# Windowed attention in a two-layer hybrid decoder: values computed with tokens on partitions, a shared tile pool, a constant kept on chip and an earlier end of the query step

## The chip, the cores and the metric

The kernel runs on one core of one Trainium2 chip. The metric is the device time of one execution in microseconds; three runs of the kernel before are known, and one more execution was profiled.

## The reference

One inference step of two layers. Each layer normalises its input, projects it with one weight matrix, and gives the parts to two groups of heads: windowed attention (8 query heads of 64, 2 key/value heads, window 128, a sink per head) and a gated delta rule (4 heads of 128 by 128). Their outputs are gated, concatenated and projected back, and the input is added. It does this for a prompt of 2048 tokens and for 8 sample sequences of 4 tokens with caches, all in float32. What the change touches is this:

```python
def _sink_attend(q, k, v, mask, sinks):
    s = einsum('...qkgd,...skd->...kgqs', q, k) * HEAD_DIM ** -0.5
    s = where(mask, s, -inf)
    m = maximum(max(s, -1), sink)
    p = exp(s - m)
    denom = sum(p, -1) + exp(sink - m)
    return einsum('...kgqs,...skd->...qkgd', p / denom, v)
```

For the prompt, a block of 128 queries sees its own block of 128 keys up to the diagonal and the previous block above the diagonal, 128 keys in all for each query; the first block of the sequence has no previous one.

## The kernel before, in words

The prompt's 2048 tokens are worked through in groups of 512 (`gi` 0 to 3), each with 4 token tiles of 128, for each of 2 layers. A group's body is a run of projections (`block`, line 484): each takes 8 or 4 pieces of weights and makes, with three float32r passes, 24 matmuls of 512 columns per output tile. Between pieces, `tk.step()` advances side tasks. Such a task is a Python generator with a number of turns and a start and an end step in the dictionary `W`: `q_task` (steps 17 to 30, 6 turns), `inv_rows` (from step 20, 33 turns, GpSimd's row by row inversion of small triangular blocks, lines 811 and 813, copied out at 817), `att_task` (24 to 47, 20 turns), `inv_task`, `qk_task`, `scan_task`, `mixd_task`, `mixa_task`. So the emitted order of work is set by these steps; a scheduler that allots tiles and places semaphores then lays down each engine's queue before the run. On the chip each queue is worked in order.

Tiles come from pools of equal buffers. `f2` gives 2 KB per partition and has 9 of them; the masked probabilities `PT`, the tanh `th`, the products `pr` of `inv_rows`, the sample's temporaries and many others live there. `f4` gives 4 KB and has 5: the raw queries `qh` (two, held until the last query transposes), `At` of `inv_rows`, the probabilities `Pt`, the inverse's `X`, `Xc`, `T2` and others. PSUM has 4 tiles for projections (`mm`) and 4 for everything else (`px`).

Weights: `fetch` (line 244) keeps 4 pieces ahead. In the first group of a layer a piece is loaded whole into `raw` (its own pool of 3, line 258 with its DMA in 259), split into a rounded half by ScalarE (line 262) and a rest by GpSimd (line 263), and written out for the other groups, which load the two halves (line 265). In the first group the sample's rows are multiplied with the same `raw` piece (line 519); in the third group the output weights are loaded whole once more for this.

Attention for a token tile `tt`, in turns: `scores(tt, 0)` makes the scores of four heads (lines 668, 669), ScalarE copies the own block's part to `Pt` and VectorE fills in the previous block's part above the diagonal (672, 673), so that `Pt` holds, for each query, its 128 keys of two blocks in one row of 128; `scores(tt, 1)` the other four; `softmax` takes the maximum, the exponentials (689) and the denominators, and multiplies `Pt` with their reciprocals (696). `turn` transposes the four heads of a key/value head on TensorE (701) and makes two masked copies on VectorE (704), one for the own block's keys and one for the previous block's. `values` multiplies with the value tiles (711):

```python
for kb in range(1 if head else 0, 2):
    for kv in range(2):
        PE.matmul(po[kv * HD:kv * HD + HD, :], vts[tt + kb][:, kv * HD:kv * HD + HD],
                  PT[kv, kb].rearrange("p a b -> p (a b)"), ...)
A.copy(g["m0"][tt // 2][:, tt % 2], po.rearrange("p (a b) -> p a b", a=4))
```

The value tile (128 keys by 64) is the stationary operand and the probabilities of four heads (512 columns) move; the result has channels on partitions, the two key/value heads on two halves of them, which is how the gate (1027) and the output projection want it. The turns of tile `tt` lie between those of tile `tt + 1`.

A sample head (`sample_head`) loads a selection matrix `sel` (128 by 256, float32) for itself, 8 times in all (line 1272), for the matmul in line 1300.

## Time and profile before

| | us |
|---|---|
| median of 3 runs | 2385.9 (2383.13 to 2389.49) |
| the profiled execution | 2384.89 |
| its span | 2383.1 |
| granted TensorE clock, mean | 0.972 |

PE is TensorE's matmuls, PEld its weight loads, DVE VectorE, ACT ScalarE, POOL GpSimd, SP the engine that issues the DMAs. "L711" is a line of the kernel before. A row of the timeline gives the start, the length of the merged stretch, the operation with what it writes and reads, how many, and in brackets the idle time of the engine before it with what ended it. A row of a group gives how many, the busy time in us, the mean ns of one, and the idle time before them. A float32 matmul that is no transpose shows as two instructions, each with its own weight load.

### The profile page before, as it was taken

To read this page: it belongs to the slowest core of one execution; us is meant where nothing else is said; L and a number is where in the kernel's file an instruction comes from. 1 tells how busy PE (TensorE), PEld (TensorE's weight loads), DVE (VectorE), ACT (ScalarE), POOL (GpSimd) and SP (SyncE) were. 2 spreads that over 40 slices of the span, in tenths; PEclk is the share of its full clock that TensorE was granted. 3 is DMA by queue.
4 is the path that set the end of the run, shared out by engine and by line. 5 is a ranking of instruction groups with operands and counts; after the bars stand their busy time and mean duration, and the time that the engine had idled before them with its cause. 6 is when DMAs were issued, how large, how long until landed. Compare 5 with 4: busy or idle time off the path is not lost.

```text
span 2383.1 us, 41057 instructions
## 1 busy us (share of the span) xinstructions
PE 2227.7 (93%) x14340; PEld 1771.6 (74%) x14340; DVE 1642.2 (69%) x5060; ACT 909.6 (38%) x2864; POOL 447.4 (19%) x732
## 2 busy tenths in 40 slices
PE   6989999879999899979999899999899989999799
PEld 5766788658887687867877677887688777788677
DVE  6677677577678764677656867778767787557663
ACT  3544523234233342334325445244432344323331
POOL 3272320400004000040023623104000130002100
PEclk9989999979999999989999999999999999999899
DMA  5654685514765348544566546854357534675236
GB/s 172 208 190 160 206 282 184 158 57 140 225 194 170 105 146 267 181 124 131 162 213 222 173 148 215 272 190 125 118 162 224 192 113 133 200 231 161 82 116 199
DMA packets 211298, 414.14 MB, mean 174 GB/s; under 512 B 61340, under 2 KB 89604, under 8 KB 211028
## 3 DMA queue, kind: packets, MB, share of 16 engines
q1 hardware_dynamic: 211092, 411.53, 53.4%
q8 instruction: 113, 1.85, 0.3%
q14 instruction: 93, 0.76, 0.1%
HBM read 312.84 MB, written 101.62 MB: 174 GB/s over the span
## 4 chain that ended last, share of the span: by engine, by line
PE 59%; DVE 8%; POOL 6%; DMA 3%; issue 2%; ACT 2%; SPq 0%; POOLq 0%; ACTq 0%; DVEq 0%
PE mm L484 40%; POOL Xh L813 3%; POOL pr L811 3%; PE px L711 2%; PE px L946 1%; PE px L954 1%; PE px L940 1%; PE px L926 1%; PE px L934 1%; PE px L701 1%; PE px L781 1%; DMA hl<-hl 1%; PE px L668 1%; PE px L519 1%; DVE vT L744 1%
## 5 line engine op out<-in xcount | busy, mean ns | idle before, releaser
L484 PE MATMUL mm<-xT,hl 128*128 128x512 f32 x3072 | 777.5, 403 | 4.1 <-POOL hl L263 3.8
L484 PEld LDWEIGHTS mm<-xT,hl 128*128 128x128 f32 x3072 | 571.0, 192 | 124.2 <-issue 6.7
L484 PE MATMUL mm<-hl,xT 128*128 128x512 f32 (+1 forms) x2304 | 511.2, 369 | 44.3 <-DVE rs_t L204 25.9
L484 PEld LDWEIGHTS mm<-hl,xT 128*128 128x128 f32 x2304 | 379.1, 192 | 114.4 <-issue 56.5
L263 POOL TENSOR_TENSOR hl<-raw,hl 128x512 fp32r<-128x512 f32 (+1 forms) x144 | 186.5, 1300 | 409.7 <-ACT hl L262 360.2
L811 POOL TENSOR_TENSOR pr<-At,Xh 128x126 f32<-128x126 f32 (+22 forms) x248 | 99.2, 400 | 580.1 <-DMA At<-ad 286.6
L484 PE MATMUL mm<-mixA,hl 128*128 128x512 f32 x768 | 187.9, 397 | 0.0
L484 PE MATMUL mm<-mixD,hl 128*128 128x512 f32 x768 | 181.6, 392 | 1.0 <-DVE mixD L970 1.0
L1029 POOL TENSOR_TENSOR mixA<-m,mixA 128x256 fp32r<-128x256 f32 x64 | 45.5, 736 | 719.2 <-ACT mixA L1028 492.7
L484 PEld LDWEIGHTS mm<-mixD,hl 128*128 128x128 f32 x768 | 142.6, 188 | 33.7 <-DVE mixD L970 1.8
L744 DVE SCALAR_TENSOR_TENSOR KQ<-mm,pc,KQ 128x511 f32<-128x511 f32 (+2 forms) x192 | 142.0, 740 | 35.1 <-ACT KQ L741 34.8
L484 PEld LDWEIGHTS mm<-mixA,hl 128*128 128x128 f32 x768 | 140.7, 188 | 30.4 <-issue 2.2
L262 ACT CAST hl<-raw 128x512 fp32r<-128x512 f32 (+1 forms) x144 | 85.0, 595 | 140.2 <-PE mm L484 76.4
L689 ACT ACTIVATE Pt<-Pt,nm 128x128 f32<-128x128 f32 x256 | 99.3, 391 | 21.5 <-DVE nm L681 21.5
L813 POOL TENSOR_TENSOR Xh<-Xh,pr 128x126 f32<-128x126 f32 (+22 forms) x248 | 103.0, 416 | 18.9
L1060 DVE TENSOR_TENSOR xr<-mm,xr 128x512 f32<-128x512 f32 x64 | 43.7, 691 | 79.6 <-PE mm L484 79.6
L672 ACT COPY Pt<-px 128x256 f32<-128x256 f32 x128 | 43.7, 374 | 143.1 <-PE px L669 110.8
L704 DVE TENSOR_TENSOR PT<-px,cst 128x512 f32<-128x512 f32 x124 | 82.1, 683 | 16.7 <-PE px L701 16.2
L701 PE MATMUL px<-cst,Pt 128*128 128x128 f32 x256 | 41.9, 289 | 41.2 <-ACT th L210 26.9
L741 ACT ACTIVATE KQ<-mm,pc 128x512 f32<-128x512 f32 x64 | 43.7, 687 | 94.0 <-PE mm L484 93.9
L668 PE MATMUL px<-kT,q 128*128 128x256 f32 (+1 forms) x256 | 72.6, 313 | 5.0 <-DVE q L650 1.7
L359 ACT CAST xT<-x 128x512 fp32r<-128x512 f32 x64 | 35.5, 618 | 93.9 <-PE mm L484 83.0
(392 smaller groups left out, 3708.7 us busy)
## 6 DMA issues: line engine op xcount, KB each, us to landing
hl<-hl SPq DMA_DIRECT2D x512, 512.0 KB
hl<-hl SPq DMA_DIRECT2D x64, 264.0 KB
raw<-in_wf_dram SPq DMA_DIRECT2D x64, 256.0 KB
raw<-in_w_out_dram SPq DMA_DIRECT2D x64, 256.0 KB
x<-in_x_prompt_dram SPq DMA_DIRECT2D x16, 512.0 KB
raw<-in_wt_dram SPq DMA_DIRECT2D x32, 256.0 KB
xr<-in_x_prompt_dram SPq DMA_DIRECT2D x32, 256.0 KB
y<-xr SPq DMA_DIRECT2D x32, 256.0 KB
```

What stands on the lines that cost most here:

```text
L262: A.copy(hl[:, 0], raw)
L263: G.tensor_sub(hl[:, 1], raw, hl[:, 0].bitcast(F32))
L484: PE.matmul(pss[u], lhs, rhs, start=(k == 0 and q == 0), stop=(k == 7 and q == 2))
L668: PE.matmul(sps[kv][:, jj, c0:], q, kT[:, kv, cols], start=True, stop=False)
L689: A.activation(Pt[:, kv, j], Pt[:, kv, j], AF.Exp, bias=nm[:, h:h + 1], scale=0.125, accum_out=den[:, h:h + 1])
L701: PE.transpose(pt[:, j, :], Pt[:, kv, j], ident)
L704: V.tensor_mul(ptt, pt, (umat if kb else slower).unsqueeze(1).to_broadcast([P, 4, P]))
L711: PE.matmul(po[kv * HD:kv * HD + HD, :], vts[tt + kb][:, kv * HD:kv * HD + HD], PT[kv, kb].rearrange("p a b -> p (a b)"), start=(kb == 0 o ...
L744: V.scalar_tensor_tensor(dest[:, d:], ps[:, 0:T - d], w, dest[:, d:], op0=ALU.mult, op1=ALU.add)
L811: G.tensor_mul(pr, At[:, j, j + 1:].unsqueeze(2).to_broadcast([P, n, m]), Xh[:, j, 0:m].unsqueeze(1).to_broadcast([P, n, m]))
L813: G.tensor_sub(Xh[:, j + 1:, 0:m], Xh[:, j + 1:, 0:m], pr)
L1029: G.tensor_sub(lo, m, hi.bitcast(F32))
```

## The change

Five edits. (1) The whole weight pieces `raw` come from the `f2` pool, which has 12 buffers instead of 9; the pool of 3 is gone. (2) `sel` is loaded once into a constant tile. (3) `q_task` runs from step 18 to 27 instead of 17 to 30. (4) `softmax` no longer multiplies `Pt`; it returns the reciprocals. `turn` makes the own block's masked copy on VectorE as before, but the previous block's part as a plain copy by ScalarE less the masked copy, subtracted on GpSimd. `values` takes the transposed probabilities of one head (128 by 128) as the stationary operand and the value tile's 64 columns as the moving one, so that the result has tokens on partitions; VectorE multiplies it with the reciprocals on the way out of PSUM; `finish` transposes it to channels on partitions on TensorE and ScalarE copies it to `m0`. (5) The values of tile `tt - 2` are emitted right after the first scores of tile `tt`, and `finish` after its second scores and softmax; there are still 20 turns.

```diff
-W = dict(k1=8, pre0=13, pre1=19, q0=17, q1=30, ir0=20, ir1=((32,) + (27,) * 3), iv0=(36, 31, 31, 31), iv1=(41, 36, 36, 36), att0=24, att1=47,
-         qk0=29, qk1=35, sc0=(41,) * 4, sc1=52, sa0=-4, sa1=30, sp0=20, sp1=50, sh0=58, shd=11, shl=13, wla=4, wraw=3, xn0=2, xn1=8, sla=3,
+W = dict(k1=8, pre0=13, pre1=19, q0=18, q1=27, ir0=20, ir1=((32,) + (27,) * 3), iv0=(36, 31, 31, 31), iv1=(41, 36, 36, 36), att0=24, att1=47,
+         qk0=29, qk1=35, sc0=(41,) * 4, sc1=52, sa0=-4, sa1=30, sp0=20, sp1=50, sh0=58, shd=11, shl=13, wla=4, xn0=2, xn1=8, sla=3,
...
     def f2(shape, dt=F32, name="f2"):
-        return f2p.tile(shape, dt, tag="f2", name=name, bufs=9)
+        return f2p.tile(shape, dt, tag="f2", name=name, bufs=12)
...
+    sel = cp.tile([P, 2, P], F32, name="sel")
...
                 if whole:
-                    raw = wp.tile([P, kk, m], F32, tag="raw", name="raw", bufs=W["wraw"])
+                    raw = f2([P, kk, m], name="raw")
                     dma(raw, src)
...
-                rd = smt([P, 8], "rd")
+                rd = smt([P, 8], "rd", 3)
                 V.reciprocal(rd, den)
-                for kv in range(2):
-                    V.tensor_mul(Pt[:, kv], Pt[:, kv], rd[:, 4 * kv:4 * kv + 4].unsqueeze(2).to_broadcast([P, 4, P]))
+                return rd
 
             def turn(tt, Pt, kv, PT):
                 pt = xt_([P, 4, P])
                 for j in range(4):
                     PE.transpose(pt[:, j, :], Pt[:, kv, j], ident)
-                for kb in range(1 if gi == 0 and tt == 0 else 0, 2):
-                    ptt = PT[kv, kb] = f2([P, 4, P], name="PT")
-                    V.tensor_mul(ptt, pt, (umat if kb else slower).unsqueeze(1).to_broadcast([P, 4, P]))
-
-            def values(tt, PT):
+                if gi or tt:
+                    pp = PT[kv, 0] = f2([P, 4, P], name="PT")
+                    A.copy(pp, pt)
+                po = PT[kv, 1] = f2([P, 4, P], name="PT")
+                V.tensor_mul(po, pt, umat.unsqueeze(1).to_broadcast([P, 4, P]))
+                if gi or tt:
+                    G.tensor_sub(pp, pp, po)
+
+            def values(tt, PT, rd):
                 head = gi == 0 and tt == 0
-                po = xt_([P, T])
-                for kb in range(1 if head else 0, 2):
-                    for kv in range(2):
-                        PE.matmul(po[kv * HD:kv * HD + HD, :], vts[tt + kb][:, kv * HD:kv * HD + HD],
-                                  PT[kv, kb].rearrange("p a b -> p (a b)"), start=(kb == 0 or head), stop=(kb == 1))
+                po = xt_([P, 4, 2, HD])
+                for kv in range(2):
+                    for j in range(4):
+                        for kb in range(1 if head else 0, 2):
+                            PE.matmul(po[:, j, kv], PT[kv, kb][:, j], vts[tt + kb][:, kv * HD:kv * HD + HD], start=(kb == 0 or head),
+                                      stop=(kb == 1))
+                o = f2([P, 4, 2, HD], name="o")
+                V.tensor_mul(o, po, rd.rearrange("p (k j) -> p j k", k=2).unsqueeze(3).to_broadcast([P, 4, 2, HD]))
+                return o
+
+            def finish(tt, o):
+                pt = xt_([P, 4, P])
+                for j in range(4):
+                    PE.transpose(pt[:, j], o[:, j].rearrange("p a d -> p (a d)"), ident)
                 if tt % 2 == 0:
                     g["m0"].append(gp.tile([P, 2, 4, P], F32, tag="q", name="m0", bufs=5))
-                A.copy(g["m0"][tt // 2][:, tt % 2], po.rearrange("p (a b) -> p a b", a=4))
+                A.copy(g["m0"][tt // 2][:, tt % 2], pt)
 
-            last = None
-            for tt in range(NT + 1):
+            Pts, PTs, rds = {}, {}, {}
+            for tt in range(NT + 2):
                 if tt < NT:
-                    Pt = f4([P, 2, 4, P], name="Pt")
-                    scores(tt, 0, Pt)
-                    yield
-                if last is not None:
-                    turn(tt - 1, last, 0, PT)
+                    Pts[tt], PTs[tt] = f4([P, 2, 4, P], name="Pt"), {}
+                    scores(tt, 0, Pts[tt])
+                if tt > 1:
+                    o = values(tt - 2, PTs[tt - 2], rds[tt - 2])
+                yield
+                if 0 < tt <= NT:
+                    turn(tt - 1, Pts[tt - 1], 0, PTs[tt - 1])
                     yield
                 if tt < NT:
-                    scores(tt, 1, Pt)
-                    softmax(Pt)
+                    scores(tt, 1, Pts[tt])
+                    rds[tt] = softmax(Pts[tt])
+                if tt > 1:
+                    finish(tt - 2, o)
+                yield
+                if 0 < tt <= NT:
+                    turn(tt - 1, Pts[tt - 1], 1, PTs[tt - 1])
                     yield
-                if last is not None:
-                    turn(tt - 1, last, 1, PT)
-                    yield
-                    values(tt - 1, PT)
-                    yield
-                last, PT = Pt, {}
...
-        sel = f2([P, 2, P], name="sel")
-        dma(sel, a["const_k"])
...
     dma(cs_s, a["const_s"])
+    dma(sel, a["const_k"])
```

## Rows read from the trace of the kernel before

**Rows 1.** The page, part 1: busy us, share, instructions

```profile
PE 2227.7 (93%) x14340; PEld 1771.6 (74%) x14340; DVE 1642.2 (69%) x5060; ACT 909.6 (38%) x2864; POOL 447.4 (19%) x732
```

**Rows 2.** Windows: busy us of PE, PEld, DVE, ACT, POOL; granted clock, DMA

```profile
400.00:500.00 100.00, 81.51 (x453) 63.69 (x453) 67.00 (x213) 32.22 (x106) 25.84 (x64) 0.86 0.42 128
...
1000.00:1100.00 100.00, 84.19 (x580) 68.14 (x579) 73.46 (x207) 37.80 (x119) 25.63 (x64) 0.93 0.38 112
...
0.00:2384.00 2384.00, 2227.70 (x14340) 1771.62 (x14340) 1642.16 (x5060) 909.61 (x2864) 447.40 (x732) 0.97 0.54 174
```

**Rows 3.** Waits of TensorE: us in total, times, longest us

```profile
PE px L701 <- ACT th L210: 26.9, 2, 13.5
PE mm L484 <- DVE rs_t L204: 25.9, 7, 5.5
PE mm L484 <- issue: 13.2, 3, 8.0
...
PE px L701 <- DVE Pt L696: 9.6, 3, 6.3
...
PE px L912 <- DVE vT L211: 5.8, 2, 4.9
...
PE mm L484 <- POOL hl L263: 3.8, 1, 3.8
```

**Rows 4.** Timeline of TensorE: one token tile's values (start us, us)

```profile
499.54 1.94 PE L711 MATMUL px<-PT,vt 128*64 128x512 f32 x8
501.41 0.46 PE L1193 MATMUL px<-cst,xx 56*128 56x56 f32 x4
```

**Rows 5.** Timeline of TensorE: nearest shapes to the new matmuls

```profile
617.97 0.94 PE L337 MATMUL px<-ones,xsq 128*128 128x1 f32 x8
...
497.42 1.06 PE L898 MATMUL px<-KQ 128*128 128x128 f32 x8
...
509.36 1.14 PE L864 MATMUL px<-Xc,AK 64*64 64x64 f32 x16
...
539.18 0.60 PE L701 MATMUL px<-cst,Pt 128*128 128x128 f32 x4
```

**Rows 6.** Groups of TensorE by shape: busy us, mean ns, idle before

```profile
L898 PE MATMUL px<-KQ 128*128 128x128 f32 x256 | 35.4, 282 | 2.8 <-ACT junk L895 1.7 <-ACT Xc L858 1.0
...
L337 PE MATMUL px<-ones,xsq 128*128 128x1 f32 x64 | 8.7, 257 | 0.7 <-DVE xsq L332 0.7
```

**Rows 7.** Groups of VectorE and GpSimd by shape

```profile
L704 DVE TENSOR_TENSOR PT<-px,cst 128x512 f32<-128x512 f32 x124 | 82.1, 683 | 16.7 <-PE px L701 16.2
...
L696 DVE TENSOR_TENSOR Pt<-Pt,rd 128x512 f32<-128x512 f32 x64 | 44.0, 729 | 0.7
...
L263 POOL TENSOR_TENSOR hl<-raw,hl 128x512 fp32r<-128x512 f32 x128 | 171.4, 1343 | 333.6 <-ACT hl L262 295.4 <-issue 20.8 <-DMA x<-in_x_prompt_dram 5.7
```

**Rows 8.** Single lines L715 and L745: duration ns min/median/max

```profile
L715 ACT COPY m<-px x32: 568/586/607, 188.7 to 2310.0; 128x512 f32<-128x512 f32 x32
...
L745 DVE SCALAR_TENSOR_TENSOR KQ<-halo,pc,KQ x192: 171/211/1251, 60.5 to 2218.6; 128x1 f32<-128x1 f32 x64, 128x2 f32<-128x2 f32 x64, 128x3 f32<-128x3 f32 x64
```

**Rows 9.** Timeline of GpSimd and VectorE, first group of layer 0

```profile
60.43 1.28 POOL L263 TENSOR_TENSOR hl<-raw,hl 128x512 fp32r<-128x512 f32 x1 [2.99 <-ACT hl L262]
...
60.54 1.18 DVE L745 SCALAR_TENSOR_TENSOR KQ<-halo,pc,KQ 128x1 f32<-128x1 f32 x1
```

**Rows 10.** Timeline of the last group of layer 0: ScalarE, GpSimd, TensorE

```profile
1046.99 0.37 ACT L672 COPY Pt<-px 128x256 f32<-128x256 f32 x1 [13.74 <-POOL pr L811]
...
1047.33 1.31 POOL L817 COPY X<-Xh 64x512 f32<-64x512 f32 x2
...
1053.06 1.09 PE L701 MATMUL px<-cst,Pt 128*128 128x128 f32 x4 [13.47 <-ACT th L210]
```

**Rows 11.** Chain that ended last: start us, us, what

```profile
1072.94 5.00 DMA Xd<-xd
```

**Rows 12.** Timeline of GpSimd in the second group of layer 0

```profile
469.08 0.33 POOL L811 TENSOR_TENSOR pr<-At,Xh 128x16 f32<-128x16 f32 x1 [6.59 <-PE px L1193]
```

## The prediction

> **What bounds the kernel now.** I read the page's busy times first. TensorE is busy for 2227.7 of 2383.1 us and VectorE for 1642.2 [rows 1]: whatever is added to TensorE's queue is paid unless a stall swallows it. The windows come next. The stretch 400:500 has TensorE at 81.5 us of 100 with a granted clock of 0.86, the stretch 1000:1100 has 84.2 and 0.93, the whole run 0.97 [rows 2]. So there is something to win in the places where attention begins, twice over, because the clock drops from its upper level (2.4 GHz) to its lower one (1.2 GHz) in them. The list of TensorE's waits says what ends the idle time [rows 3]: the transposes of the probabilities (L701) behind ScalarE's tanh, 26.9 us in two waits; the projections (L484) behind VectorE's rsqrt, 25.9 us; the same behind "issue", 13.2; L701 behind the normalisation L696, 9.6; L912 behind VectorE, 5.8. These five make 81.4 us, and they are the stalls that the change can touch.
>
> **Values, on TensorE (the largest term).** Now a token tile takes 4 matmuls of 512 moving columns, each two instructions: 8 instructions from 499.54 to 501.41, 1.87 us [rows 4]. Eight times 512 columns go by in that time because the two kv heads write different column halves of the array and run in pairs. The code makes 30 full tiles and two half ones (the first tile of a layer has no earlier keys), 31 x 1.87 = 58.0 us. The change makes 16 matmuls a tile, 32 instructions, each with 128x128 probabilities as the stationary operand and 64 columns moving: 30 x 32 + 2 x 16 = 992. No row has this shape. From both sides, each stretch less the length of one instruction, 0.26 to 0.28 us [rows 5, 6]: L337 moves one column over a 128-column stationary operand, 8 in 0.94 us, (0.94 - 0.26)/7 = 0.097 us each; L898 moves 128, 8 in 1.06 us, (1.06 - 0.28)/7 = 0.111; L864 moves 64 columns over a stationary operand of only 64, 16 in 1.14 us, (1.14 - 0.26)/15 = 0.059. Going from 1 to 128 moving columns hardly matters, halving the stationary operand does: the weight load sets the pace, and the new matmuls have the full one. I take 0.111: 110.1 us. Low end 992 x 0.059 = 58.5, if loads hide under neighbouring projections. So +52.1 us, low end +0.5.
>
> The Trainium skill speaks of this in TensorE: Matmul & The Clock Gate, section Back-to-back issue gap: a sustained stream of load and matmul pairs takes about 81 ns each at 128 columns. By that figure the 992 would take 80.4 us, an estimate, and the final sum would come out at 2381 instead of 2411. The trace disagrees for this data type, with 0.111 us at the same 128 columns [rows 5], and the measurement decides.
>
> **The turn back.** The new result has tokens on partitions, so `finish` transposes it: 4 per tile, 128 in all. L701 does four in 0.60 us, (0.60 - 0.27)/3 = 0.11 each [rows 5, 6]: +14.1 us. TensorE's queue grows by 66.2 us. Nothing hides this where TensorE runs without a gap, which is most of the tiles' time.
>
> **VectorE, ScalarE, GpSimd.** L696 goes, 44.0 us. Of the 124 masked copies L704 60 go, 60 x 0.683 = 41.0; 32 scalings of 128x512 from PSUM come, at L704's price 21.9. VectorE: -63.1 us. ScalarE gets 60 copies of 128x512 from PSUM, at L715's 0.586 us 35.2 us; it is far from full. GpSimd gets 60 subtractions of that size, at L263's 1.343 us 80.6 us [rows 7, 8]. All of it lies beside TensorE; its worth is what it does to the stalls. And there the subtraction costs VectorE something: while GpSimd subtracts at 60.43, VectorE's one-column L745 takes 1.18 us against its median of 0.211 [rows 8, 9]. Bounds for 60 subtractions: nothing (VectorE idle, or reading PSUM) and 60 x 0.97 = 58 us. I take half, 29, since about half of VectorE's work in attention reads PSUM in the code; VectorE then gains 34 us, not 63.
>
> **The waits, one by one.** (a) The transposes need no normalised probabilities any more: of the 9.6 us behind L696 in three waits I take off 6, three times a pass of two L696 at 0.73 and the small steps ahead of them. Bounds 0 and -9.6. (b) In the last group of a layer ScalarE stood 13.74 us until GpSimd's row sweep let go of `At`, because the second tile of scores was put in At's 4 KB tile; X is copied only at 1047.33; TensorE stood 13.47 us [rows 10]. With q done three steps sooner (27, not 30) both q tiles are free before the second scores. But the order of work keeps GpSimd late: the next that needs it is the reload of Xd, which alone stood 5.0 us on the chain [rows 11], and VectorE's transposes of Xd stand in a strict queue. I take off half, 2 x 7 = 14; bounds 0 and -27. (c) In the second group GpSimd waited 6.59 us for a 2 KB tile that L1193 still read [rows 12]; with 12 tiles instead of 9, and no weights sharing them outside the first and third group, this goes: -6, bounds 0 and -6.6. (d) The 25.9 and 5.8 us behind VectorE: its net gain is 34 us over 32 tiles, about 1 us in each such wait, but the values move two turns later and leave these waits less filled. -8, bounds +10 and -25. (e) Clock: the run misses 3% of it [rows 2], some 72 us; with 34 of the 155 us idle gone a fifth of it, 16, and I put over half of that into time in which TensorE stood anyway: -6; bounds 0 and -16.
>
> **Edits at nothing.** Seven of the eight loads of `sel`, 128 KB each, leave SP's queue; none is on TensorE's path. The q step is denser: each of its four turns issues 4 transposes, 2 casts on ScalarE and 2 subtractions on VectorE, past GpSimd's row sweep and no DMA; VectorE's slack covers it, and if it is gone a turn costs about 1.4 us. Raw weights now compete with temporaries for 12 tiles and SP waits in order for the tile; weights are asked for four pieces ahead, so I take nothing; the upper bound is +30 us, if each of the eight token tiles of the first groups costs one late piece at the 3.8 us of the one that L484 waited for now [rows 3]. New waits: the values wait for GpSimd's subtraction, with the projections queued behind them on TensorE; two turns of distance cover that.
>
> **Sum.** The profiled execution took 2384.9 us (span 2383.1 and 1.8 around it), 1.0 under the median of the three runs. 2384.9 + 66.2 - 6 - 14 - 6 - 8 - 6 = 2411.1, rounded 2411. All ends of the waits at once give 2367 and 2461; halfway to both, 2389 to 2436, is the forecast's own range. The low end of the values takes 52 us from the sum, 2359; late weights in full make it 2441.
>
> **Rivals.**
> 1. *The stalls give back more than the values take.* One cause for all of them: engines that are late against an order laid down beforehand, GpSimd's sweep and VectorE's queue above all, and the change takes work out of just that stretch. If those five waits went [rows 3], 81.4 us, and with them a third of the missing clock, 24 us, the time would be 2384.9 + 66.2 - 105 = 2346. For it: the waits sit where VectorE's 63 us are saved. Against: a sweep that is late stays late. It decides from 66 us of relief on; 59 to 73 us give 2385, 7 more or less.
> 2. *GpSimd's subtractions take VectorE's gain away.* By rows a VectorE operation can be held for nearly the whole subtraction [rows 9]; if that holds for all 60, VectorE loses 80.6 us where it saved 63.1 and is 17 us later, so that (d) is gone and 17 are added: 2411 + 8 + 17 = 2436. The Trainium skill, SBUF — State Buffer, section SBUF: two separate sides, has it as a lock: the pair of ports is held for a whole instruction and the other engine stands. The trace agrees where both operands lie in SBUF (1.18 against 0.211) [rows 8, 9]. Against the full price: not every operation of VectorE is of the kind that gets held.
> 3. *The q step frees nothing* and the 13.5 us waits stay: 2411 + 14 = 2425, inside the forecast.
>
> **Chances.** Forecast (rival 3 with it) 0.45; rival 2, 0.13; both slower by over 0.3%, about 7 us, which is what a measurement of this kernel can tell from no change. Rival 1 in full or in large part 0.28, faster. Relief about as large as the cost 0.14, the same. Slower 0.58, same 0.14, faster 0.28. Most chance lies over two signs, so the forecast's own 2389 to 2436 stands beside the range that should hold 8 in 10: 2358 to 2445, which leaves out rival 1's far end and the case where late weights come on top.
>
> **What would show it.** Right: new value matmuls 992 at a spacing near 0.111 us; `finish` 128; VectorE's busy time down by 30 to 45 us, with short two-operand VectorE work lengthened beside GpSimd's new line; TensorE's idle time down by less than 66 us. Wrong: idle time below 90 us with a clock above 0.985 (rival 1); a spacing of 0.06 to 0.08; or VectorE's busy time no lower than before with longer rsqrt waits (rival 2).

## The result, and the profile after

Eight runs of each kernel on the same chip: 2404.87 us after (2394.74 to 2412.56), 2387.58 before (2383.13 to 2389.98). The ratio is 1.0076, 95% interval 1.0056 to 1.0095: slower, by 17.3 us. The eight times of the kernel after spread over 18 us, those of before over 7. The profiled execution took 2408.9 us, 4.0 above its median, so rows of this trace that add up to a sum are read against 2408.9.

Page, part 1, of the kernel after, against [rows 1]:

```profile
PE 2284.1 (95%) x15212; PEld 1884.7 (78%) x15212; DVE 1580.7 (66%) x4968; ACT 942.2 (39%) x2924; POOL 507.5 (21%) x792
```

TensorE is 56.4 us busier, VectorE 61.5 us less, ScalarE 32.6 and GpSimd 60.1 us more. TensorE's time outside work (span less busy) went from 155.4 us to 2407.1 - 2284.1 = 123.0. So TensorE took on 56 us and gave 32 us of idle time back; the difference, 24 us, is how much longer this execution's span is.

The same three windows as [rows 2], in the kernel after (busy us of PE, PEld, DVE, ACT, POOL, then the granted clock):

```profile
400.00:500.00 100.00, 98.81 (x642) 80.28 (x641) 74.20 (x231) 42.23 (x150) 27.46 (x66) 1.00 0.49 148
1000.00:1100.00 100.00, 94.27 (x646) 80.20 (x644) 75.14 (x218) 45.68 (x159) 29.15 (x67) 0.93 0.40 119
...
0.00:2408.00 2408.00, 2284.05 (x15212) 1884.65 (x15212) 1580.69 (x4968) 942.21 (x2924) 507.51 (x792) 0.98 0.53 172
```

The two holes in which attention began are filled: 98.8 us of 100 instead of 81.5, with the clock never off its upper level (2.4 GHz) in the first, and 94.3 instead of 84.2 in the second.

TensorE's waits, against [rows 3] (us in total, times, longest):

```profile
PE px L520 <- DMA raw<-in_wf_dram: 18.4, 15, 2.7
PE px L379 <- DVE xst L374: 14.6, 1, 14.6
PE mm L485 <- DVE rs_t L204: 14.6, 3, 6.1
PE mm L485 <- DVE rs_t L205: 9.7, 2, 4.8
...
PE px L338 <- DVE xsq L333: 4.9, 1, 4.9
```

The 26.9 us behind ScalarE's tanh, the 13.2 behind "issue" (idle time for which the profile shows no releaser) and the 9.6 behind the normalisation have left the top of the list. At its head stands a wait that came to 1.4 us in four waits before: the sample's matmul waits for a whole weight piece, now 18.4 us in 15 waits for one kind of piece and 20.9 in 18 with the output weights'.

The new work by form (count, busy us, mean ns, idle time before):

```profile
L716 PE MATMUL px<-vt,PT 128*128 128x64 f32 x992 | 124.4, 285 | 0.0
L725 PE MATMUL px<-cst,o 128*128 128x128 f32 x128 | 19.7, 273 | 0.0
L704 ACT COPY PT<-px 128x512 f32<-128x512 f32 x60 | 34.7, 581 | 152.9 <-PE px L701 150.0
L706 DVE TENSOR_TENSOR PT<-px,cst 128x512 f32<-128x512 f32 x64 | 43.8, 687 | 29.0 <-ACT PT L704 22.9 <-DMA raw<-in_wt_dram 3.4 <-issue 0.7
L708 POOL TENSOR_TENSOR PT<-PT 128x512 f32<-128x512 f32 x60 | 76.9, 1285 | 548.2 <-DVE PT L706 466.7 <-DVE rs_t L204 35.7 <-DVE rs_t L205 19.7
L719 DVE TENSOR_TENSOR o<-px,rd 128x512 f32<-128x512 f32 x32 | 22.1, 692 | 91.6 <-PE px L716 87.5
```

All counts are those of the prediction, and the durations are within 5% of it: 581 ns for the copy, 1285 for the subtraction, 692 for the scaling.

**Where along the run it went.** The 6912 projection matmuls (L484 before, L485 after) are the same in every kernel here. Number them in order of time; the start of the k-th in one trace less its start in another is how late the one kernel is at that point, and the step from group to group (864 matmuls) is what a group costs. Worked out from the start times of those records, in us, for groups 0 to 3 of each layer (the last one up to the end of the span). Each row compares two single executions, so its sum can differ by some us from that of the medians:

```
                                        layer 0                     layer 1
                                   0      1      2      3      0      1      2      3    sum
before -> after                 19.9  -14.4    0.5    0.8    7.5    5.2    3.7    0.9   24.0
before -> q step alone           2.5   -9.2    1.1  -10.2    2.3   -2.4   -0.5  -10.9  -27.3
before -> shared tiles alone    16.4  -18.8    2.5   -1.4    2.2    4.3    0.4   -1.2    4.4
before -> new attention alone    7.0    7.5    3.4    3.5    9.8    7.6    6.3    4.1   49.4
e4 (nine tiles) -> after         7.2  -56.6   -3.3    5.1    3.6    1.3   -7.3    6.7  -43.4
after -> values twice            8.7   15.7   13.9    8.5   19.1   12.3   10.9   18.8  108.0
```

The first row is what the change did; the others belong to the experiments below. Attention costs something in every group; the two other edits act in a few places, with both signs.

### The profile page after: what moved, and what is told of

Same layout as the page of the kernel before. It is cut to its first block, busy times and chain, and to the rows that moved or that the text cites. A ratio compares the mean times of both kernels' runs of the same rounds, so it can differ in the third digit from the quotient of the medians.

```text
span 2407.1 us, 42958 instructions
## 1 busy us (share of the span) xinstructions
PE 2284.1 (95%) x15212; PEld 1884.7 (78%) x15212; DVE 1580.7 (66%) x4968; ACT 942.2 (39%) x2924; POOL 507.5 (21%) x792
## 4 chain that ended last, share of the span: by engine, by line
PE 69%; DVE 10%; DMA 8%; POOL 5%; ACT 3%; issue 3%; SPq 1%; POOLq 0%; ACTq 0%; DVEq 0%
PE mm L485 45%; PE px L716 5%; DMA raw<-in_wf_dram 3%; POOL Xh L827 2%; DMA raw<-in_w_out_dram 2%; POOL hl L264 2%; POOL pr L825 1%; PE px L520 1%; PE px L954 1%; DVE KQ L758 1%; PE px L948 1%; PE px L701 1%; PE px L940 1%; DMA Xd<-xd 1%; PE px L960 1%
## 5 line engine op out<-in xcount | busy, mean ns | idle before, releaser
L485 PE MATMUL mm<-xT,hl 128*128 128x512 f32 x3072 | 777.4, 402 | 11.1 <-POOL hl L264 4.7
L485 PEld LDWEIGHTS mm<-xT,hl 128*128 128x128 f32 x3072 | 566.7, 191 | 130.2 <-POOL hl L264 7.3
L485 PE MATMUL mm<-hl,xT 128*128 128x512 f32 (+1 forms) x2304 | 508.3, 368 | 28.6 <-DVE rs_t L204 14.6
L485 PEld LDWEIGHTS mm<-hl,xT 128*128 128x128 f32 x2304 | 378.5, 191 | 92.7 <-issue 24.3
L825 POOL TENSOR_TENSOR pr<-At,Xh 128x126 f32<-128x126 f32 (+22 forms) x248 | 93.0, 375 | 600.1 <-DMA At<-ad 173.3
L708 POOL TENSOR_TENSOR PT<-PT 128x512 f32<-128x512 f32 x60 | 76.9, 1285 | 548.2 <-DVE PT L706 466.7
L485 PE MATMUL mm<-mixA,hl 128*128 128x512 f32 x768 | 187.1, 396 | 0.8 <-POOL hl L264 0.7
L485 PE MATMUL mm<-mixD,hl 128*128 128x512 f32 x768 | 183.8, 394 | 1.6 <-ACT mixD L983 1.6
L485 PEld LDWEIGHTS mm<-mixD,hl 128*128 128x128 f32 x768 | 142.1, 188 | 34.8 <-issue 3.6
L485 PEld LDWEIGHTS mm<-mixA,hl 128*128 128x128 f32 x768 | 141.0, 188 | 30.8 <-POOL hl L264 1.6
L716 PEld LDWEIGHTS px<-vt,PT 128*128 128x128 f32 x992 | 123.5, 203 | 3.6 <-issue 0.6
L716 PE MATMUL px<-vt,PT 128*128 128x64 f32 x992 | 124.4, 285 | 0.0
L263 ACT CAST hl<-raw 128x512 fp32r<-128x512 f32 (+1 forms) x144 | 83.9, 597 | 102.4 <-DMA raw<-in_wf_dram 48.2
L690 ACT ACTIVATE Pt<-Pt,nm 128x128 f32<-128x128 f32 x256 | 99.1, 390 | 17.3 <-DVE nm L682 15.7
L827 POOL TENSOR_TENSOR Xh<-Xh,pr 128x126 f32<-128x126 f32 (+22 forms) x248 | 97.7, 394 | 19.0
L704 ACT COPY PT<-px 128x512 f32<-128x512 f32 x60 | 34.7, 581 | 152.9 <-PE px L701 150.0
L719 DVE TENSOR_TENSOR o<-px,rd 128x512 f32<-128x512 f32 x32 | 22.1, 692 | 91.6 <-PE px L716 87.5
```

What stands on the lines that cost most here:

```text
L263: A.copy(hl[:, 0], raw)
L485: PE.matmul(pss[u], lhs, rhs, start=(k == 0 and q == 0), stop=(k == 7 and q == 2))
L690: A.activation(Pt[:, kv, j], Pt[:, kv, j], AF.Exp, bias=nm[:, h:h + 1], scale=0.125, accum_out=den[:, h:h + 1])
L708: G.tensor_sub(pp, pp, po)
L716: PE.matmul(po[:, j, kv], PT[kv, kb][:, j], vts[tt + kb][:, kv * HD:kv * HD + HD], start=(kb == 0 or head), stop=(kb == 1))
L825: G.tensor_mul(pr, At[:, j, j + 1:].unsqueeze(2).to_broadcast([P, n, m]), Xh[:, j, 0:m].unsqueeze(1).to_broadcast([P, n, m]))
```

## The experiments

Times are medians, with the range of their runs, and the ratio to the kernel before on the same chip. The experiments ran on four chips (e1 to e4, e5 to e8, e9 to e11, e12), on which the kernel before took 2387.6, 2385.4, 2385.8 and 2387.1 us. Where two kernels from different chips are compared, some 2 us can be the chip's; "each against the before of its own chip" takes that out.

### One edit undone, one alone

**e1: the change with attention as before** (edits 4 and 5 undone; shared tiles, kept `sel` and the q step stay).

```diff
+                for kv in range(2):
+                    V.tensor_mul(Pt[:, kv], Pt[:, kv], rd[:, 4 * kv:4 * kv + 4].unsqueeze(2).to_broadcast([P, 4, P]))
...
-                    A.copy(pp, pt)
...
-                            PE.matmul(po[:, j, kv], PT[kv, kb][:, j], vts[tt + kb][:, kv * HD:kv * HD + HD], start=(kb == 0 or head),
+                        PE.matmul(po[kv * HD:kv * HD + HD, :], vts[tt + kb][:, kv * HD:kv * HD + HD],
```

> The changed kernel with attention as it was before (probabilities normalised, two masked copies on VectorE, value tiles stationary, no finish); the shared tiles, the kept sel and the q step from 18 to 27 stay. Theory A, what was predicted: the values and the turn back cost TensorE 66 us, and of the relief only the lighter chain of attention (waits a and d, 14 us together) belongs to attention itself; the rest belongs to q and the tiles. Then 2404.9 - 66 + 14 = 2353 us (2340 to 2365), faster than both kernels, with the 13.5 us waits of L701 in the last groups still gone. Theory B: the relief of some 42 us comes from VectorE's lighter load and the shorter chain, and q and the tiles are worth nothing: 2404.9 - 66 + 42 = 2381, the time of the kernel before.

Measured: 2356.75 us (2354.91 to 2359.35), ratio 0.9874 (0.9859 to 0.9888). Without the new attention the change would have been 30.8 us faster than before; the attention costs 48.1 us on top of the other edits.

**e2: the kernel before with the new attention alone** (edits 4 and 5; the reverse of the diff above on the other base).

> The kernel before with the new attention alone (token by token, scaled on leaving PSUM, GpSimd's subtraction, the new order of turns); raw keeps its own three tiles, 9 shared ones, sel is loaded each time, q from 17 to 30. Theory A: 2387.6 + 66 - 14 = 2440 us (2430 to 2450), with the 13.5 us waits in the last groups still there. Theory B: 2387.6 + 66 - 42 = 2412, and those waits gone or shortened although q is as before.

Measured: 2431.57 us (2428.54 to 2434.21), ratio 1.0182 (1.0165 to 1.0199): +44.0 us by itself. Its page, part 1, and the wait of TensorE that heads its list:

```profile
PE 2286.0 (94%) x15212; PEld 1882.2 (77%) x15212; DVE 1599.4 (66%) x4968; ACT 946.9 (39%) x2924; POOL 520.9 (21%) x792
```

```profile
PE px L700 <- ACT Pt L689: 22.3, 2, 11.2
```

VectorE is 42.8 us less busy, and that does not help here: the two long stalls in front of the transposes of the probabilities are still there, 22.3 us in two waits, only that they now end at the exponential.

**e3: the change with q at 17 to 30 again.**

```diff
-W = dict(k1=8, pre0=13, pre1=19, q0=18, q1=27, ir0=20,
+W = dict(k1=8, pre0=13, pre1=19, q0=17, q1=30, ir0=20,
```

> The changed kernel with the q step at 17 to 30 as before and nothing else. Theory A: the second scores of the last group wait again for At; between half and the whole of two waits of 13.5 us and a few us of clock come back: 2404.9 + 14 to 2404.9 + 32, 2419 to 2437 us. Theory B: q frees nothing that matters, 2405 within 7.

Measured: 2435.41 us (2432.48 to 2436.74), ratio 1.0201 (1.0185 to 1.0216), 30.5 us over the kernel after. The stalls come back, and with nothing else changed they are the same pair as in e2:

```profile
PE px L701 <- ACT Pt L690: 21.9, 2, 11.1
```

**e5: the kernel before with the q step alone** (18 to 27, the same line as in e3).

> The kernel before with the q step at 18 to 27 and nothing else. Theory A: an earlier q frees its two tiles for the second scores whatever else is there, the two 13.5 us waits go: 2387.6 - 28 = 2360 us (2353 to 2367). Theory C, after the surprise that the changed kernel with nine tiles took 2447.9: q sooner pays only with twelve shared tiles, and with nine it makes the second group of layer 0 wait for tiles (waits of L646, L485 and the sample's matmuls, 30 us and more between 430 and 540): 2387.6 + 16 = 2404 or more.

Measured: 2356.67 us (2354.97 to 2359.45), ratio 0.9877 (0.9862 to 0.9892): 28.7 us less than before, from two numbers in one line. The table says where: 10.2 and 10.9 us in the last group of either layer, as predicted in kind, and 9.2 in the second group of layer 0, where nothing had been put down for it. GpSimd's wait behind L1193 [rows 12] is still there in that group, and longer (14.6 us instead of 6.6). The wait of ScalarE behind GpSimd's `pr` [rows 10] is gone from this trace, and no wait of that size took its place.

**e6: the kernel before with shared tiles and kept `sel` alone** (edits 1 and 2).

```diff
-        return f2p.tile(shape, dt, tag="f2", name=name, bufs=9)
+        return f2p.tile(shape, dt, tag="f2", name=name, bufs=12)
...
-                    raw = wp.tile([P, kk, m], F32, tag="raw", name="raw", bufs=W["wraw"])
+                    raw = f2([P, kk, m], name="raw")
```

> Attention and q as before; only the twelve shared tiles and the kept sel of the change. Theory A: the 6.6 us wait of GpSimd in the second group goes and loads of raw come late in the first groups, 2387.6 - 7 + 14 = 2395 us (2385 to 2400), the 13.5 us waits stay. Theory C: the same here; what parts the theories is the sum with the q step alone: A has the two effects add up to the 30.8 us by which the changed kernel without its attention was faster, C has them add up to far less.

Measured: 2387.08 us (2384.57 to 2390.53, ten runs), ratio 1.0003 (0.9993 to 1.0013). No difference; yet it is the sum of two that are easily seen. The second group of layer 0 in the kernel before and in e6 (windows, columns as above) and, ahead of that, the one long stall in it before, from the timeline of TensorE:

```profile
490.18 1.19 PE L484 MATMUL mm<-hl,xT 128*128 128x512 f32 x2 [7.99 <-issue]
```

```profile
340.00:646.00 306.00, 281.59 (x1748) 227.25 (x1747) 207.56 (x709) 105.54 (x347) 31.98 (x74) 0.94 0.50 158
```

```profile
356.00:643.00 287.00, 276.89 (x1745) 222.49 (x1744) 206.99 (x709) 104.95 (x346) 32.92 (x74) 0.99 0.51 163
```

With more tiles GpSimd's wait of 6.6 us behind L1193 [rows 12] goes, the stall of TensorE of 8.0 us goes and the clock rises from 0.94 to 0.99; the group takes 18.8 us less by the table. What it wins there it has lost in the first group, 16.4 us. TensorE's waits in that first group of e6:

```profile
PE px L379 <- DVE xst L374: 14.8, 1, 14.8
PE mm L485 <- POOL hl L264: 5.7, 6, 1.8
PE px L338 <- DVE xsq L333: 5.0, 1, 5.0
...
PE px L520 <- DMA raw<-in_wf_dram: 3.7, 5, 1.2
PE mm L485 <- ACT hl L263: 3.6, 3, 2.3
```

The start of the kernel is later (14.8 and 5.0, against one wait of 11.8 before): the first projection matmul comes 7.3 us later than before, so that 7.3 of the 16.4 us are the start. In the rest, pieces of weights and their halves come late. What the DMA queue of SP waited for most in the first group, before and then in e6 (window 0:360):

```profile
SPq L259 <- PE px L519: 119.3, 37, 13.7
```

```profile
SPq L274 <- POOL hl L264: 132.8, 48, 13.2
```

Before, SP stands ahead of the loads of `raw`, until TensorE lets go of one of the three tiles. In e6 it stands ahead of the writes of the halves, which wait for GpSimd's remainder, and all its waits ahead of loads of `raw` make 19 us.

**e4: the change with nine tiles and `raw` in its own pool of 3** (edit 1 undone).

```diff
-        return f2p.tile(shape, dt, tag="f2", name=name, bufs=12)
+        return f2p.tile(shape, dt, tag="f2", name=name, bufs=9)
...
-                    raw = f2([P, kk, m], name="raw")
+                    raw = wp.tile([P, kk, m], F32, tag="raw", name="raw", bufs=3)
```

> The changed kernel with the whole weights in a pool of their own with three tiles and nine shared tiles, as before; sel, q and attention as changed. The changed kernel's trace has TensorE wait 20.9 us for loads of raw at the sample's matmuls (18 waits), where the kernel before had 1.4. Theory A': this is the price of sharing, the loads come late because a shared tile frees later: the waits go and the time is 2404.9 - 10 to - 20, 2385 to 2395 us. Rival: with nine tiles the temporaries wait instead (GpSimd's 6.6 us in the second group, and the like in the others), and the time is the same or up to 10 us longer, 2405 to 2415.

Measured: 2447.93 us (2445.16 to 2452.27), ratio 1.0256 (1.0238 to 1.0275), 43 us over the kernel after. Neither theory had that. TensorE's waits for `raw` do fall, from 20.9 us to 3.1. But the table has all of the loss, and more, in one place: 56.6 us in the second group of layer 0, while the first group is 7.2 us shorter, 5.8 of it ahead of the first projection. The stretch 400:560 in the kernel after, then in e4:

```profile
400.00:560.00 160.00, 153.58 (x1115) 126.70 (x1114) 112.77 (x360) 68.46 (x243) 33.87 (x71) 0.98 0.42 133
```

```profile
400.00:560.00 160.00, 121.70 (x785) 95.84 (x783) 81.72 (x262) 44.96 (x160) 27.98 (x66) 0.80 0.32 97
```

TensorE works 32 us less in this stretch, and at a granted clock of 0.80. What the engines of e4 waited for in it, from the timelines of SP, GpSimd, ScalarE, VectorE and TensorE, in order of time:

```profile
423.19 32.23 SPq L266 DMA_DIRECT2D hl<-hl  x5
...
437.33 0.69 PE L646 MATMUL px<-cst,qh 128*128 128x128 f32 x2 [7.37 <-DVE qh L404]
...
486.70 0.48 SPq L819 DMA_DIRECT2D At<-ad  x1
...
493.01 0.24 POOL L825 TENSOR_TENSOR pr<-At,Xh 128x31 f32<-128x31 f32 x1 [144.17 <-DMA At<-ad]
...
497.42 0.63 ACT L211 ACTIVATE th<-KQ 128x512 f32<-128x512 f32 x1 [26.18 <-POOL Xh L827]
...
499.21 0.42 DVE L1168 COPY ao<-px 128x256 f32<-128x256 f32 x1 [24.06 <-POOL Xh L827]
...
499.78 0.66 PE L1174 MATMUL px<-cst,ao 128*128 128x128 f32 x2 [8.04 <-DVE ao L1168]
```

Neither the tanh nor the copy `ao` reads `Xh`. Both write a 2 KB tile, and the releaser in the brackets says that the one they were given is still in use by GpSimd's sweep, which can't begin because `At` is loaded only at 486.70. In the kernel after the same two rows read

```profile
434.17 0.47 SPq L819 DMA_DIRECT2D At<-ad  x1
```

```profile
440.27 0.24 POOL L825 TENSOR_TENSOR pr<-At,Xh 128x31 f32<-128x31 f32 x1 [86.29 <-DMA At<-ad]
```

so the sweep starts 52.7 us later in e4. Why `At` comes that late can be followed some steps back. `At` is read back from `ad`; the last store of `ad` (L802) is issued at 467.67 in e4 and at 428.55 in the kernel after. In e4 it stands in SP's queue behind loads of weights (L266), five of which take from 423.19 to 455.42, because they wait for TensorE (longest wait 22.0 us; 8.5 after). TensorE stood 7.37 us behind the q step's work on VectorE just then, and its granted clock in 430:455 is 0.66, against 1.00 after. This was read, not tried, and what makes that work late with nine tiles stays open. Nor was a `raw` pool of 3 beside twelve tiles tried.

The eight corners of attention, q step and tiles (us; before 2387.6, the others as above):

```
                     q 17 to 30          q 18 to 27
                     9 tiles   12        9 tiles   12
old attention        2387.6  2387.1      2356.7  2356.8
new attention        2431.6  2435.4      2447.9  2404.9
```

The q step is worth 29 to 31 us in three of the four pairs and costs 16 in the one with new attention and nine tiles. Twelve tiles are worth nothing in two pairs, cost 4 us in a third (its ranges overlap) and are worth 43 in the one with new attention and early q. So the two edits need each other only under the new attention, and the table has the loss in one group of eight. "12" stands for the tiles and the kept `sel` together, except in the last pair: e4, at 2447.9, has nine tiles and keeps `sel`.

### What the new attention's 48 us are made of

**e9: the change with the old value matmuls** (probabilities normalised, four matmuls of 512 columns, no scaling, no `finish`; the order of the turns, ScalarE's copy and GpSimd's subtraction stay).

```diff
+                for kv in range(2):
+                    V.tensor_mul(Pt[:, kv], Pt[:, kv], rd[:, 4 * kv:4 * kv + 4].unsqueeze(2).to_broadcast([P, 4, P]))
...
-                            PE.matmul(po[:, j, kv], PT[kv, kb][:, j], vts[tt + kb][:, kv * HD:kv * HD + HD], start=(kb == 0 or head),
+                        PE.matmul(po[kv * HD:kv * HD + HD, :], vts[tt + kb][:, kv * HD:kv * HD + HD],
...
+            def finish(tt, o):
+                pass
```

> The changed kernel with the values as before (normalised probabilities move in 512 columns over the value tiles, the result with channels on partitions, no scaling on leaving PSUM, no finish), but with the changed order of turns, the changed masks and all else as changed. Theory A: the matmuls of the values and the turn back are the cost, the new order is neutral, and the time is that of the changed kernel with attention undone but the masks on ScalarE and GpSimd: 2363 us (2356 to 2370). Rival: the later values and the new order hold tiles longer and cost by themselves: 2375 to 2390, and the matmuls only the rest.

Measured: 2371.1 us (2368.37 to 2378.04), ratio 0.9943 (0.9921 to 0.9965). Between the theory and its rival. The token by token values with their scaling and their turn back, in place of the old ones with the normalisation, cost 33.8 us (32.0, each against the before of its own chip).

**e7: e1 with the previous block's mask on ScalarE and GpSimd.**

```diff
-                for kb in range(1 if gi == 0 and tt == 0 else 0, 2):
-                    ptt = PT[kv, kb] = f2([P, 4, P], name="PT")
-                    V.tensor_mul(ptt, pt, (umat if kb else slower).unsqueeze(1).to_broadcast([P, 4, P]))
+                if gi or tt:
+                    pp = PT[kv, 0] = f2([P, 4, P], name="PT")
+                    A.copy(pp, pt)
...
+                    G.tensor_sub(pp, pp, po)
```

> The changed kernel with attention as before except that the previous block's part is made as in the change: a copy by ScalarE, from which GpSimd subtracts VectorE's masked copy. It takes 41 us from VectorE and puts 77 us on GpSimd. Theory A, half of the subtraction's time holds VectorE: a gain of up to 8 us in the waits behind VectorE's rsqrt (21.5 us in six waits), 2356.8 - 4 = 2353 (2346 to 2358). Rival, the lock takes it all: 2357 to 2370, with VectorE's busy time down by less than 20 us.

Measured: 2363.3 us (2360.59 to 2365.56), ratio 0.9903 (0.9888 to 0.9918): 6.6 us slower than e1 (8.7, each against the before of its own chip). The gain of Theory A is not there; the rival's range and its sign, less than 20 us off VectorE, are. Page, part 1, of e1, then of e7:

```profile
PE 2218.7 (94%) x14340; PEld 1761.8 (75%) x14340; DVE 1620.9 (69%) x5060; ACT 913.0 (39%) x2864; POOL 435.0 (18%) x732
```

```profile
PE 2232.9 (95%) x14340; PEld 1771.0 (75%) x14340; DVE 1614.7 (68%) x5000; ACT 942.9 (40%) x2924; POOL 510.7 (22%) x792
```

Sixty masks of 0.683 us, 41.0 us, left VectorE, and it is 6.2 us less busy. Its other instructions are longer. The normalisation in e7, from the single line's durations (min, median, max), and one such place in e7's timeline:

```profile
L697 DVE TENSOR_TENSOR Pt<-Pt,rd x64: 679/686/1783, 160.9 to 2269.4; 128x512 f32<-128x512 f32 x64
```

```profile
543.82 2.35 DVE L697 TENSOR_TENSOR Pt<-Pt,rd 128x512 f32<-128x512 f32 x2
544.04 1.58 POOL L709 TENSOR_TENSOR PT<-PT 128x512 f32<-128x512 f32 x1 [4.81 <-DVE PT L707]
```

Two of them take 2.35 us where two medians make 1.37, and GpSimd's subtraction, itself 1.58 instead of a median of 1.29, lies right in it.

**e8: the change with both masks on VectorE** (the reverse edit, on the kernel after).

> The changed kernel with both masked copies on VectorE as before, no copy by ScalarE and no subtraction by GpSimd; everything else as changed. Theory A: VectorE gets back 41 us and loses some 20 to 30 us of being held: 2404.9 + 4, 2400 to 2413. Rival, the lock takes it all: 2404.9 or up to 10 us less, with VectorE's busy time up by less than 20 us.

Measured: 2398.26 us (2391.11 to 2404.49), ratio 1.005 (1.0032 to 1.0067), 6.6 us faster than the change. Page, part 1:

```profile
PE 2272.6 (95%) x15212; PEld 1872.6 (78%) x15212; DVE 1603.5 (67%) x5028; ACT 911.7 (38%) x2864; POOL 428.8 (18%) x732
```

VectorE gets 41 us of masks back and is 22.8 us busier: the subtractions had been taking 18 us from it. That is less time than Theory A had and a larger rise of VectorE's busy time than its rival had. Both pairs of medians differ by 6.6 us, which is in part chance: each against the before of its own chip, the differences are 8.7 and 4.4, and the runs of e8 and of the kernel after overlap (up to 2404.49 and from 2394.74); those of e1 and e7 don't. So the masks on the other engines cost a few us, shown clearly in the first pair alone.

From e1 in steps: masks on the other engines (e7) +6.6, the later order of the values (e9) +7.8, the values themselves +33.8; together 48.2. Each against the before of its own chip: 8.7, 7.4 and 32.0.

**e10: every value matmul issued twice**, with the sum begun afresh the second time.

```diff
-                for kv in range(2):
+                for kv in [0, 1] * 2:
```

> The changed kernel with every value matmul issued twice, 992 instructions more with weight loads of 128 columns; nothing is left out. Theory A: they are paid at the pace of the weight load wherever TensorE has no gap, 992 x 0.111 = 110 us: 2404.9 + 110 = 2515 us (2500 to 2520). Rival: part of it hides in TensorE's remaining idle time, or the loads hide under neighbouring projections, 0.06 us each: 2404.9 + 60 = 2465.

Measured: 2517.67 us (2516.47 to 2519.39), ratio 1.0553 (1.0536 to 1.0571): 112.8 us for 992 more, 0.114 us each. The page has TensorE's busy time up by 111.4:

```profile
PE 2395.5 (95%) x16204; PEld 1998.2 (79%) x16204; DVE 1581.8 (63%) x4968; ACT 943.2 (38%) x2924; POOL 507.3 (20%) x792
```

Every group of the table pays, 8.5 to 19.1 us. What was added to TensorE's queue here was paid in full: its idle time fell by 3.4 us only, from 123.0 to 119.6.

### What is better than both

**e11: the kernel before with q at 18 to 25; e12: e1 with the same.**

```diff
-W = dict(k1=8, pre0=13, pre1=19, q0=17, q1=30, ir0=20,
+W = dict(k1=8, pre0=13, pre1=19, q0=18, q1=25, ir0=20,
```

> The kernel before with the q step at 18 to 25, two steps sooner still than the change has it, to see whether the best of the versions so far (the q step alone at 18 to 27, 2356.7) has an edge to it. Theory A: once both q tiles are free before the second scores nothing more is to be had: 2357 (2350 to 2364). Rival 1: the first scores wait for q too, and the time falls to 2345. Rival 2: four turns of q in fewer steps crowd VectorE, whose rsqrt waits grow: 2365 and more.

> Attention as before, the twelve shared tiles and the kept sel of the change, and the q step at 18 to 25: the candidate for the best version. The tiles alone made no difference (2387.1), and with q at 27 none either (2356.8 with them, 2356.7 without). Theory A, tiles and old attention do not meet: 2351 us (2347 to 2355), no better than the q step at 25 alone. Rival: with q denser still, temporaries are shorter of tiles and the twelve pay: 2340 to 2346.

Measured: e11 2350.94 us (2350.05 to 2355.91), ratio 0.9853 (0.9834 to 0.9872); e12 2351.82 us (2349.13 to 2358.95), ratio 0.9856 (0.9832 to 0.9879). Two steps sooner still are worth 5.7 us more, close to what these runs can tell: the ranges of e5 and e11 overlap, and 2350.9 is still inside what Theory A allowed for no further gain. Twelve tiles add nothing under the old attention. The version to keep is e11, one line against the kernel before.

## Why the prediction was right

Slower was right, and the 2411 us lay 6 above the median. The order of the causes was right too: values on TensorE cost more than the stalls give back. That it came so near is luck: against the experiments, the q step's relief was put some 15 us too small and the attention's net cost 4 to 8 too high, while the 6 for the tiles and the 6 for the clock, which no experiment shows besides, work the other way. TensorE's idle time shows the same. The waits (a) to (d) together said 34 us, and it fell by 32.4; but the five waits of [rows 3] that the prediction named fell from 81.4 us to 27.8, by 53.6, and new waits of some 27 us came (19.5 for `raw`, 7 at the start), for which it had nothing.

**Values and turn back, +66.2 us: right.** A block of 32 value matmuls, and one of 16 in the first tile, in the timeline of TensorE after:

```profile
194.61 1.90 PE L716 MATMUL px<-vt,PT 128*128 128x64 f32 x16
...
496.52 3.68 PE L716 MATMUL px<-vt,PT 128*128 128x64 f32 x32
```

By the prediction's own way of reading, (3.68 - 0.285)/31 = 0.110 and (1.90 - 0.285)/15 = 0.108 us each, against the 0.111 taken from a row with 128 moving columns [rows 5]. Choosing the row by its stationary operand and not by its moving columns was the right choice, and e10 confirms it with 0.114 paid. With all three terms together, TensorE is 65.4 us busier after than in e1, which has the same tiles and q step, and 56.6 busier than in e9. The Trainium skill's 81 ns a pair (TensorE: Matmul & The Clock Gate, section Back-to-back issue gap) does not hold for these float32 pairs: at 0.081 the second set of 992 would have cost 80 us, an estimate from that figure, and it cost 112.8.

**What the attention gives back, (a) and (d), -14 of 66: about right as a sum, not in its parts.** The sum said +52 net of them; measured +44.0 alone and +48.1 beside the other edits. By e9 and e7 the values and their scaling cost only 33.8 of the 48, though their price on TensorE is right, while the masks and the later order, from which the prediction expected relief (d), cost some 14. The two errors nearly cancel. (a) TensorE's waits behind the normalisation are gone from its list. (d) The waits behind VectorE's rsqrt and `vT` were 25.9 + 5.8 us and are 14.6 + 9.7 + 3.5: 4 us of relief where 8 stood. The rest of what came back is spread over many small gaps and isn't settled further. VectorE's own gain was put at 30 to 45 us: it is 42.8 with the attention alone, but 61.5 for the whole change, for which the sign was given, so that this sign failed. The two other edits take 8 to 9 us each from its busy time besides (1634.3 in e5, 1633.1 in e6, against 1642.2), and the prediction had nothing for that.

**(b) The q step, -14 us: wrong in size, by half.** The step said that the 13.5 us stalls would only be halved, because GpSimd stays late and the reload of `Xd` or VectorE's queue would be late next. In the last group of layer 0 after, from TensorE's timeline:

```profile
1049.94 0.60 PE L701 MATMUL px<-cst,Pt 128*128 128x128 f32 x4
...
1059.99 0.50 PE L485 MATMUL mm<-xT,hl 128*128 128x512 f32 x1 [2.66 <-DMA hl<-hl]
...
1070.05 1.20 PE L854 MATMUL px<-Xd,AK 32*32 32x32 f32 x64 [1.37 <-DMA Xd<-xd]
```

The transposes wait for nothing and the reload of `Xd` holds TensorE for 1.37 us. No next stall of size stood behind the first. By e5 the step is worth 28.7 us, clock included: 21 in the two last groups, and 9 in the second group of layer 0, a place that the prediction had given to the tiles alone.

**(c) and the edits at nothing: wrong.** The relief in the second group was real and larger than the 6 us put down (18.8 in e6). The late weights, taken as nothing with a bound of 30, were real too: 16.4 us in the first group of e6, 7.3 of them a later start. The one cancels the other, so that the pair measured nothing where -6 stood. The rule that four pieces ahead cover a late load was the false step. The prediction's reason for a late load, SP in line for a tile that a temporary holds, is the smaller part of what the trace shows: 19 us of SP's waits in e6's first group, against 132.8 ahead of the writes of the halves, which stand in the same queue. No run parts the two, nor the later start from the shared pool.

**That the edits add up** was never put as a step, and it is the assumption that the runs break. The parts measured alone, 2387.6 + 44.0 - 28.7 and nothing for the tiles, give 2403 and the change gives 2405; but attention and q step without the tiles (e4, which keeps `sel`) give 2447.9 where the same addition says 2403. So the addition holds for the change because the twelve tiles are there.

**Clock, -6 us.** The mean granted clock rose from 0.972 to 0.979; its worth can't be told apart from that of the stalls with which it rose.

**The rivals.** Rival 1 (idle time below 90 us, a clock above 0.985) did not occur; the idle time is 123.0. One part of it shows in e5, where nothing was added to TensorE: the relief from the stalls and their clock was twice the forecast's, by another order alone, with no work taken out. Rival 2 is true in its mechanism and wrong in its size. The subtraction does take away from VectorE (35 of 41 us in e7, 18 of 41 in e8, with 29 taken) and moving the masks is a loss of a few us. It never became 25: VectorE's busy time doesn't set the end here (e2 has 42.8 us less of it and takes 44.0 longer). The Trainium skill's lock (SBUF — State Buffer, section SBUF: two separate sides) agrees with e7's timeline, where two operations beside a subtraction take 2.35 us instead of 1.37. Rival 3, that the q step frees nothing, is refuted by e3 and e5.

## What to carry to other kernels

Price a new matmul by the nearest row with the same stationary operand, and price an edit of the order of work by trying it alone: one line of this change, the q step, won 29 us, nearly what the new values lost (33.8). An edit that measures nothing may be the sum of a gain and a loss in different stretches; the lateness of the same instruction in two traces shows them. Where temporaries share a pool of tiles with the operands of a slow engine, look at who holds the next tile, not only at how much work each engine has.

## What was not expected of the hardware

GpSimd's subtraction holds even short operations of VectorE, also one with a single tensor operand (L693). In the kernel after, from the timeline:

```profile
1054.30 2.54 POOL L708 TENSOR_TENSOR PT<-PT 128x512 f32<-128x512 f32 x2
...
1054.44 1.17 DVE L692 TENSOR_TENSOR den<-den,es 128x8 f32<-128x8 f32 x1 [1.40 <-ACT Pt L690]
...
1055.64 1.22 DVE L693 TENSOR_SCALAR den<-den 128x8 f32<-128x8 f32 x1
```

Two operations on 8 columns take 1.17 and 1.22 us beside two subtractions, and the second ends 0.02 us after its subtraction. It has a median of 0.170 us in the same trace, is lengthened like this in 2 of its 32 instances, and never takes more than 0.173 in e1, where nothing is subtracted for attention. Both lie on the way to the reciprocals that the scaling needs.

The eight runs of the kernel after also spread over 18 us, the four of e10, the same kernel with more matmuls, over 3. Nothing here explains that.
